# A causal convolution moved from VectorE to TensorE: 72 fp32 products over four token phases

## The chip, the cores and the metric

The kernel runs on one core of one Trainium2 chip, in one launch. The metric is the device time of a run in microseconds (us). One execution of each kernel is also recorded by the hardware profiler; all durations below come from that one execution.

## The reference, cut to what matters

The reference is a small decoder: 512 tokens, 1024 channels, two attention layers, then a block that mixes three kinds of token mixers, then an MLP. The change touches one of the three mixers, the convolution module. Its input `u` is 512 tokens by 512 channels:

```python
def conv_module(u, cv_w, cv_b, ln_w, ln_b):
    a, b = jnp.split(u, 2, axis=-1)
    h = a * jax.nn.sigmoid(b)                       # 512 tokens x 256 channels
    h = lax.conv_general_dilated(h, cv_w[:, None, :], window_strides=(1,),
        padding=[(CV_WIDTH_FILTER - 1, 0)],         # 31 taps, causal
        dimension_numbers=('NWC', 'WIO', 'NWC'),
        feature_group_count=CV_WIDTH) + cv_b        # each channel by itself
    hf = h.astype(f32)
    mu = jnp.mean(hf, axis=-1, keepdims=True)
    var = jnp.mean(jnp.square(hf - mu), axis=-1, keepdims=True)
    hf = (hf - mu) * lax.rsqrt(var + EPS) * ln_w + ln_b
    return jax.nn.silu(hf)
```

The result is concatenated with that of the two other mixers (a gated linear recurrence with four heads, and a sparse attention with four heads) and goes through one output matrix of 1024 by 1024.

## The kernel before, in words

Every large product is done as three fp32r products on TensorE: both operands are split in a high and a low part (`wh`/`wl` for weights, by `load_group` on lines 250 to 268; ScalarE casts `wh`, and VectorE or GpSimd subtracts for `wl`). Weights arrive in 512 KB pieces `raw` on SyncE's DMA queue, with three `raw` buffers and four of each `wh` and `wl`.

The mixers' part of the kernel is written as units: Python generators that issue a piece of work each. The list `ORDER` (line 1182) says in which order the units are issued: `iq`, `sv`, `sN`, `tN` (scores and top-k selection of the sparse attention), `fN`, `vN` (gates and values of a pair of recurrence heads), `hN` (one recurrence head, nine levels, each a chain of VectorE, GpSimd, ScalarE and TensorE), `cu` (projection to the convolution's input, `glu`), `cN` (convolution of channel half N), `sqk` and `dN` (queries and keys, then attention for a pair of heads), `ln` (layer norm and silu of the convolution). The framework then fixes one static order of instructions for each engine out of this list by priority and expected readiness, so that instructions of several units alternate on an engine; on the chip each engine goes through its own list in order, and an instruction that waits holds up all that stands behind it on that engine.

The convolution before (`u_cv`, lines 1141 to 1152): channels are on the partitions, 512 tokens along the free axis, in two halves of 128 channels. A half is one multiplication by the last tap (line 1148) and 30 instructions of multiply and add on VectorE (line 1151, recorded as line 118, which is the helper `stt`), each over 482 to 511 tokens, and a ScalarE instruction that adds the bias (line 1152). `u_ln` (line 1154) transposes the result to tokens on the partitions (`ptc`, eight transposes), takes mean and variance there, transposes back (`ptd`) and applies the silu.

Buffers that matter: tag `s8` has 12 buffers of 8 KB a partition, tag `s4` 7 buffers of 4 KB, tag `w2` 7 of 2 KB, tag `pt` 3 buffers (the probabilities `PT` of the attention and `AT` of a recurrence head share them), and the PSUM tag `mm` three banks. Helpers that record many operations on one line: line 111 and 112 (`ts`), 115 (`tt`), 118 (`stt`), 273 to 275 (the three products of `mm3`).

## Time and profile before

| what | value |
|---|---|
| median of 3 runs | 1347.48 us (1343.02 to 1352.38) |
| the profiled execution's own time | 1343.12 us |
| its span, first to last instruction | 1341.3 us |
| TensorE busy / VectorE busy / ScalarE busy / GpSimd busy | 1237.7 / 843.4 / 586.7 / 355.6 us |
| mean granted TensorE clock | 0.97 of full speed |

The profile cuts the span in 40 slices of 33.5 us; each digit of the busy line is the busy share of a slice in tenths. In the rows further down, times are us from the start of the span unless marked ns. The operation `cv<-glu,cols,cv` is the convolution. A bracket at the end of a timeline row gives the idle time of the engine before the row, and what ended it. Some fp32 products appear as two MATMUL records each: a head's ten products `Oh` of line 1046 give 20 records, a transpose gives one.

### The profile page before, as it was taken

To read this page: it belongs to the slowest core of one execution; us is meant where nothing else is said; L and a number is where in the kernel's file an instruction comes from. 1 tells how busy PE (TensorE), PEld (TensorE's weight loads), DVE (VectorE), ACT (ScalarE), POOL (GpSimd) and SP (SyncE) were. 2 spreads that over 40 slices of the span, in tenths; PEclk is the share of its full clock that TensorE was granted. 3 is DMA by queue.
4 is the path that set the end of the run, shared out by engine and by line. 5 is a ranking of instruction groups with operands and counts; after the bars stand their busy time and mean duration, and the time that the engine had idled before them with its cause. 6 is when DMAs were issued, how large, how long until landed. Compare 5 with 4: busy or idle time off the path is not lost.

```text
span 1341.3 us, 18014 instructions
## 1 busy us (share of the span) xinstructions
PE 1237.7 (92%) x6596; PEld 1010.0 (75%) x6596; DVE 843.4 (63%) x1638; ACT 586.7 (44%) x1196; POOL 355.6 (27%) x434
## 2 busy tenths in 40 slices
PE   5999998999999989999987787988999999999997
PEld 4677777878877868889765666766797888888886
DVE  5647656766467689544899889876586244353444
ACT  4544553553256656326564334644352322131222
POOL 1304202110134240003475755245111010015211
PEclk9999999999999999999999888978999999999999
DMA  5234325424441244343222201030364233234221
GB/s 199 66 124 132 124 96 160 144 70 145 162 134 61 67 142 152 92 144 111 64 69 93 78 18 63 23 108 1 110 219 158 81 124 104 85 110 156 95 79 64
DMA packets 42024, 141.73 MB, mean 106 GB/s; under 512 B 4928, under 2 KB 5824, under 8 KB 41936
## 3 DMA queue, kind: packets, MB, share of 16 engines
q1 hardware_dynamic: 36144, 126.06, 29.0%
q10 hardware_dynamic: 5792, 14.52, 3.1%
q8 instruction: 52, 0.85, 0.3%
q14 instruction: 36, 0.29, 0.1%
HBM read 132.14 MB, written 8.42 MB: 105 GB/s over the span
## 4 chain that ended last, share of the span: by engine, by line
PE 51%; DVE 16%; issue 6%; POOL 5%; ACT 3%; DMA 2%; ACTq 0%; POOLq 0%; DVEq 0%
PE psw L275 4%; PE psw L273 4%; PE psw L274 4%; PE psf L275 4%; PE psf L273 4%; PE psf L274 4%; DVE X L115 2%; PE pso L274 2%; PE pso L275 2%; PE pso L273 2%; PE psg L275 2%; POOL wl L115 2%; PE O L554 2%; PE psg L274 2%; PE psg L273 2%
## 5 line engine op out<-in xcount | busy, mean ns | idle before, releaser
L259 ACT ACTIVATE wh<-raw 128x1024 fp32r<-128x1024 f32 (+2 forms) x138 | 141.9, 1036 | 158.5 <-PE psw L275 50.5
L115 DVE TENSOR_TENSOR wl<-raw,wh 128x1024 fp32r<-128x1024 f32 x104 | 129.8, 1261 | 58.9 <-ACT wh L259 56.7
L115 POOL TENSOR_TENSOR wl<-raw,wh 128x1024 fp32r<-128x1024 f32 (+2 forms) x34 | 76.9, 2281 | 49.4 <-ACT wh L259 49.2
L115 POOL TENSOR_TENSOR hnr<-hnr,mhalf 128x8 f32<-128x8 f32 (+1 forms) x28 | 49.6, 1771 | 152.3 <-DVE hnr L111 141.5
L1261 POOL TENSOR_SCALAR acth<-sqf 128x512 fp32r<-128x512 f32 x32 | 22.9, 718 | 240.3 <-DVE sqf L115 240.3
L274 PE MATMUL psf<-xfl,wh 128*128 128x512 f32 (+1 forms) x232 | 85.5, 369 | 0.4 <-DVE xfl L118 0.4
L275 PE MATMUL psf<-xfh,wl 128*128 128x512 f32 (+1 forms) x232 | 85.3, 368 | 0.1
L273 PE MATMUL psf<-xfh,wh 128*128 128x512 f32 (+1 forms) x232 | 84.5, 367 | 0.0
L273 PE MATMUL psw<-wh,acth 128*128 128x512 f32 (+1 forms) x206 | 79.0, 383 | 0.0
L275 PE MATMUL psw<-wh,actl 128*128 128x512 f32 (+1 forms) x206 | 78.9, 383 | 0.0
L274 PE MATMUL psw<-wl,acth 128*128 128x512 f32 (+1 forms) x206 | 78.9, 383 | 0.0
L519 ACT ACTIVATE PT<-ptp 128x512 f32<-128x512 f32 (+3 forms) x96 | 45.6, 481 | 43.9 <-PE ptp L548 30.8
L336 DVE CUSTOM_DVE_ANT_0 adaw<-adaw,cact 128x1024 f32<-128x1024 f32 x48 | 58.3, 1230 | 5.0 <-DMA adaw<-in_ada 4.8
L511 ACT ACTIVATE P<-Sp,nm 128x128 f32<-128x128 f32 (+3 forms) x80 | 44.5, 557 | 30.5 <-DVE nm L509 30.2
L273 PE MATMUL psq<-wh,xah 128*128 128x512 f32 x128 | 53.2, 415 | 0.9 <-ACT xah L294 0.9
L275 PE MATMUL psq<-wh,xal 128*128 128x512 f32 x128 | 53.2, 415 | 0.2 <-DVE xal L115 0.2
L274 PE MATMUL psq<-wl,xah 128*128 128x512 f32 x128 | 52.9, 413 | 0.0
L118 DVE SCALAR_TENSOR_TENSOR cv<-glu,cols,cv 128x482 f32<-128x482 f32 (+29 forms) x60 | 50.9, 848 | 0.5
L275 PEld LDWEIGHTS psf<-xfh,wl 128*128 128x128 f32 x232 | 43.7, 188 | 7.9 <-DVE wl L115 0.8
L274 PEld LDWEIGHTS psf<-xfl,wh 128*128 128x128 f32 x232 | 43.7, 188 | 7.9 <-DVE xfl L118 0.6
L273 PEld LDWEIGHTS psf<-xfh,wh 128*128 128x128 f32 x232 | 43.5, 188 | 7.2
L554 PEld LDWEIGHTS O<-v,PT 128*128 128x128 f32 x320 | 42.7, 192 | 7.6 <-ACT PT L519 5.4
(522 smaller groups left out, 3596.3 us busy)
## 6 DMA issues: line engine op xcount, KB each, us to landing
raw<-in_w SPq DMA_DIRECT2D x56, 512.0 KB, 3.6
adaw<-in_ada SPq DMA_DIRECT2D x48, 512.0 KB, 4.2
raw<-in_wa SPq DMA_DIRECT2D x32, 512.0 KB, 4.3
raw<-in_w2m SPq DMA_DIRECT2D x32, 512.0 KB, 4.5
raw<-in_wb SPq DMA_DIRECT2D x16, 512.0 KB, 4.7
ck<-cd ACTq DMA_DIRECT2D x16, 256.0 KB, 4.3
raw<-in_woa SPq DMA_DIRECT2D x8, 512.0 KB, 4.9
raw<-in_wob SPq DMA_DIRECT2D x8, 512.0 KB, 4.4
```

The lines of the kernel that those rows point to most:

```text
L115: return note(eng, eng.tensor_tensor(o, x, y, op=op))
L118: return note(ve, ve.scalar_tensor_tensor(o, x, s, y, op0=op0, op1=op1, **kw))
L259: i = ac.activation(wh, r, AF.Copy), tt(gp if len(res) in (gpa if gpl is None else gpl) else ve, wl, r, wh.bitcast(F32), ALU.subtract)
L273: te.matmul(o, lh, rh, start=i == 0, stop=False)
L274: te.matmul(o, lh, rl, start=False, stop=False)
L275: te.matmul(o, ll, rh, start=False, stop=i == n - 1)
L336: i = ve.tensor_tensor_reduce(w, w, ada["c"], 1.0, 0.0, op0=ALU.mult, op1=ALU.add, accum_out=mod[:, j:j + 1])
L511: ac.activation(P[:, :n], Sp[:, :n], AF.Exp, bias=nm, scale=-1.0, accum_out=l)
L519: ac.activation(o, i, AF.Copy)
L554: te.matmul(O[:, i, s], PT[s][:, j], v[:, j, (2 * p + s) * 64:(2 * p + s + 1) * 64], start=j == 0, stop=j == i)
L1261: gp.tensor_scalar(xh, s, 1.0, 0.0, op0=ALU.mult, op1=ALU.add)
```

## The change

The convolution becomes products on TensorE. Tokens are split in four phases (token = 4t + r) and channels in eight groups of 32. For one group, the partitions hold (phase r, channel c), and the free axis holds t, with eight columns of zeros in front: this is `gph`. A product takes 128 consecutive columns of `gph` as the stationary operand, and a table `T` as the moving one: `T` has, for four consecutive tap positions, the tap of channel c on the diagonal of a 32 by 32 block and zeros elsewhere. Nine such products, summed in PSUM, give all 31 taps for 128 t, four phases and 32 channels; eight groups make 72 products. The result has tokens on the partitions, so the layer norm reads it without the eight `ptc` transposes.

- `conv_consts` (new unit `xc`, after `t2`): zeroes on GpSimd, 16 small DMAs on SyncE's queue that write the taps shifted by phase (`wtap`), a scaling by 0.5 and the 32-wide identity `id32` on GpSimd, two transposes on TensorE and a ScalarE copy for the bias row.
- `u_cu`: `glu` is written by phase, and 16 DMAs on SyncE's queue carry it to `gph`.
- `u_cv(m)`: called with m = 1 first, as before; the first call builds `tap8` on VectorE; each call builds four tables `T` of 128 x 1024 on VectorE, issues 36 products into one `mm` bank, and adds the bias on VectorE.
- `u_ln`: no `ptc`; statistics from SBUF, the result of the normalisation in place.
- `ORDER`: `xc` is added; `c0` and `ln` stand earlier.

```diff
@@ -1062,7 +1062,30 @@
         yield
 
     siw = const.tile([128, 4, 8], F32, name="siw")
-    svw = qst = kst = glu = sqk = cv = None
+    svw = qst = kst = glu = sqk = cv = tap8 = None
+
+
+    cvx = S8([128, 2048], F32, "cvx")
+    gph = cvx[:, 0:1088].rearrange("p (g t) -> p g t", t=136)
+    wtap = cvx[:, 1088:1376].rearrange("p (g x) -> p g x", x=36)
+    brow = cvx[:, 1376:1632].rearrange("p (m c) -> p m c", c=128)
+    id32 = cvx[:, 1632:1664]
+
+    def conv_consts():
+        gp.memset(gph[:, :, 0:8], 0.0)
+        gp.memset(wtap, 0.0)
+        o = COLS["cvw"][0]
+        for r in range(4):
+            for q in range(4):
+                sy.dma_start(wtap[32 * r:32 * r + 32, q:8:4, 5 - r:36 - r],
+                             a["cols"][32 * q:32 * q + 32, o:o + 62].rearrange("p (m j) -> p m j", j=31))
+        gp.tensor_scalar(wtap, wtap, 0.5, 0.0, op0=ALU.mult, op1=ALU.add)
+        tt(gp, id32, idc[:, 0:32], idc[:, 32:64], ALU.add)
+        pt = PM("ptm", (128, 4, 128), "tt")
+        for m in range(2):
+            te.transpose(pt[:, m], col("cvb", m).to_broadcast([128, 128]), ident)
+        ac.activation(brow, pt[:, 0:2], AF.Copy)
+
 
     def u_sv():
         nonlocal svw
@@ -1105,7 +1128,7 @@
         nonlocal glu
 
         wc = load_group(a["w2"][1], gpl=gpc)
-        glu = S4([128, 2, 512], "glu")
+        glu = S4([128, 2, 4, 128], "glu")
         psa = []
         for m in (2, 3, 0, 1):
             ps = PM("psc")
@@ -1115,7 +1138,11 @@
                 ac.activation(t, ps, AF.Tanh, scale=0.5)
                 psa.append(t)
             else:
-                stt(glu[:, m], psa[m], 1.0, ps, ALU.add, ALU.mult)
+                v = lambda x: x.rearrange("p (t r) -> p t r", r=4)
+                stt(glu[:, m].rearrange("p r t -> p t r"), v(psa[m]), 1.0, v(ps), ALU.add, ALU.mult)
+        for r in range(4):
+            for q in range(4):
+                sy.dma_start(gph[32 * r:32 * r + 32, q:8:4, 8:136], glu[32 * q:32 * q + 32, :, r])
 
     def u_sqk():
         nonlocal sqk
@@ -1138,48 +1165,51 @@
             mix_out(1, p, pt.rearrange("p a b -> p (a b)"))
             yield
 
-    def u_cv(ms=(0, 1)):
-        nonlocal cv
+    def u_cv(m):
+        nonlocal cv, tap8
 
         if cv is None:
-            cv = S4([128, 2, 512], "cv")
-        for m in ms:
-            w0 = COLS["cvw"][0] + 31 * m
-            ts(ve, cv[:, m], glu[:, m], cols[:, w0 + 30:w0 + 31], ALU.mult)
-            for j in range(30):
-                d = 30 - j
-                stt(cv[:, m, d:512], glu[:, m, 0:512 - d], cols[:, w0 + j:w0 + j + 1], cv[:, m, d:512], ALU.mult, ALU.add)
-            ac.activation(cv[:, m], cv[:, m], AF.Identity, bias=col("cvb", m), scale=0.5)
+            cv = S4([128, 4, 8, 32], "cv")
+            tap8 = S4([128, 8, 4, 32], "tap8")
+            tt(ve, tap8, wtap[:, :, 32:36, None].to_broadcast([128, 8, 4, 32]),
+               id32[:, None, None, :].to_broadcast([128, 8, 4, 32]), ALU.mult)
+        ps = PM("pcv", (128, 4, 4, 32))
+        for g in range(4):
+            gg = 4 * m + g
+            T = S4([128, 32, 32], "taps")
+            tt(ve, T, wtap[:, gg, 0:32, None].to_broadcast([128, 32, 32]), id32[:, None, :].to_broadcast([128, 32, 32]),
+               ALU.mult)
+            for u in range(9):
+                w = T[:, 4 * u:4 * u + 4] if u < 8 else tap8[:, gg]
+                te.matmul(ps[:, g].rearrange("p a b -> p (a b)"), gph[:, gg, u:u + 128], w.rearrange("p a b -> p (a b)"),
+                          start=u == 0, stop=u == 8)
+        bias = brow[:, m].rearrange("p (g c) -> p g c", c=32)
+        tt(ve, cv[:, :, 4 * m:4 * m + 4].rearrange("p q g c -> p g q c"), ps,
+           bias[:, :, None, :].to_broadcast([128, 4, 4, 32]), ALU.add)
 
     def u_ln():
-        ct = S4([128, 4, 256], "ct")
-        for q in range(2):
-            pt = PM("ptc", (128, 2, 2, 128), "tt")
-            for t2 in range(2):
-                for m in range(2):
-                    tb = 2 * q + t2
-                    te.transpose(pt[:, t2, m], cv[:, m, tb * 128:(tb + 1) * 128], ident)
-            for t2 in range(2):
-                tb = 2 * q + t2
-                st = SM(6, "bst")
-                x = pt[:, t2].rearrange("p a b -> p (a b)")
-                ve.bn_stats(st, x)
-                mv = SM(2, "bmv")
-                ve.bn_aggr(mv, st)
-                rr = rstd(mv[:, 1:2], 1, "rrc")
-                ts(ve, ct[:, tb], x, mv[:, 0:1], ALU.subtract, rr, ALU.mult)
+
+        ct = cv.rearrange("p q g c -> p q (g c)")
+        for q in range(4):
+            st = SM(6, "bst")
+            ve.bn_stats(st, ct[:, q])
+            mv = SM(2, "bmv")
+            ve.bn_aggr(mv, st)
+            rr = rstd(mv[:, 1:2], 1, "rrc")
+            ts(ve, ct[:, q], ct[:, q], mv[:, 0:1], ALU.subtract, rr, ALU.mult)
         for m in range(2):
             pt = PM("ptd", (128, 4, 128), "tt")
-            for tb in range(4):
-                te.transpose(pt[:, tb], ct[:, tb, m * 128:(m + 1) * 128], ident)
+            for q in range(4):
+                te.transpose(pt[:, 3 - q], ct[:, q, m * 128:(m + 1) * 128], ident)
             zz = W2("zz")
-            ac.activation(zz, pt.rearrange("p a b -> p (a b)"), AF.Identity, bias=col("lnb", m), scale=col("lnw", m))
+            ac.activation(zz.rearrange("p (t q) -> p q t", q=4), pt, AF.Identity, bias=col("lnb", m),
+                          scale=col("lnw", m))
             th = W2("th")
             ac.activation(th, zz, AF.Tanh, scale=0.5)
             stt(zz, th, 1.0, zz, ALU.add, ALU.mult)
             mix_out(1, 2 + m, zz, 0.5)
 
-    ORDER = "iq sv s2 s3 f0 f0 f0 s1 v0 v0 t2 f1 f1 f1 cu h1 h1 t3 h0 h1 h0 c1 sqk h1 h0 t1 sqk h0 v1 d1 d1 d1 d1 d1 d0 v1 d0 d0 d0 c0 h2 h2 h2 ln h3 d0 h3 h3 h2 h3".split()
+    ORDER = "iq sv s2 s3 f0 f0 f0 s1 v0 v0 t2 xc f1 f1 f1 cu h1 h1 t3 h0 h1 h0 c1 sqk h1 h0 t1 sqk h0 v1 c0 d1 d1 d1 d1 d1 d0 v1 d0 d0 d0 ln h2 h2 h2 h3 d0 h3 h3 h2 h3".split()
... 
     g1 = mod_row(2, "g1")
```

## Rows read from the trace of the kernel before

**Rows 1.** The page, first part: busy time, share of the span, instructions.

```profile
PE 1237.7 (92%) x6596; PEld 1010.0 (75%) x6596; DVE 843.4 (63%) x1638; ACT 586.7 (44%) x1196; POOL 355.6 (27%) x434
```

**Rows 2.** Stretches: us; busy PE, PEld, DVE, ACT, POOL; clock, DMA share, GB/s.

```profile
787.00:839.00 52.00, 40.84 (x224) 32.91 (x224) 46.46 (x72) 20.57 (x47) 24.60 (x29) 0.84 0.13 41
839.00:890.00 51.00, 45.62 (x261) 37.04 (x260) 42.38 (x86) 29.41 (x81) 13.75 (x18) 0.90 0.26 83
890.00:942.00 52.00, 42.85 (x363) 32.47 (x362) 34.83 (x76) 25.19 (x62) 28.69 (x36) 0.84 0.01 4
```

**Rows 3.** Chain that ended last, shares by line: of 787:839, then of 890:942.

```profile
by line: DVE cv L118 30.5%; DVE X L115 12.1%; PE psA L1035 7.9%; PE psA L993 5.3%; PE Oh L1046 4.3%; DVE hhr L111 4.3%; DVE Qs L118 3.8%; DVE KLs L118 3.8%; POOL X L115 3.5%; PE pshi L275 3.4%; PE pt L458 2.9%; PE pshi L273 2.6%; PE pshi L2
...
by line: DVE X L115 28.2%; issue 14.3%; PE psA L993 10.3%; PE Oh L1046 5.6%; DVE D L1020 5.5%; POOL hhr L115 3.9%; PE psA L1035 3.3%; DVE xm L118 3.1%; DVE zz L118 2.6%; ACT sq L1053 2.4%; PE psA L1030 2.2%; PE psA L1025 2.1%; PE pso L275 1
```

**Rows 4.** Groups on VectorE, 640:960: xcount | busy us, mean ns | idle before.

```profile
L118 DVE SCALAR_TENSOR_TENSOR cv<-glu,cols,cv 128x482 f32<-128x482 f32 (+29 forms) x60 | 50.9, 848 | 0.5
...
L115 DVE TENSOR_TENSOR wl<-raw,wh 128x1024 fp32r<-128x1024 f32 x6 | 7.2, 1215 | 0.5 <-ACT wh L259 0.5
...
L115 DVE TENSOR_TENSOR on<-Oh,gg 128x512 f32<-128x512 f32 x4 | 2.7, 685 | 0.1
...
L111 DVE TENSOR_SCALAR cv<-glu,cols 128x512 f32<-128x512 f32 x2 | 1.0, 476 | 0.0
```

**Rows 5.** Timeline of TensorE, 812:836: start, duration, record, idle before.

```profile
816.16 0.65 PE L1025 MATMUL psA<-X 128*64 128x64 f32 x8 [3.25 <-DVE X L115]
...
822.63 0.40 PE L274 MATMUL pshi<-wl,xch 128*128 128x512 f32 x1
822.86 0.40 PE L275 MATMUL pshi<-wh,xcl 128*128 128x512 f32 x1
...
828.87 2.05 PE L1035 MATMUL psA<-X 128*128 128x256 f32 x4 [4.46 <-DVE X L115]
...
831.14 0.63 PE L273 MATMUL pshi<-wh,xch 128*128 128x512 f32 x1
831.57 0.63 PE L274 MATMUL pshi<-wl,xch 128*128 128x512 f32 x1
```

**Rows 6.** Timeline of TensorE: products of a recurrence head at full clock.

```profile
803.20 0.83 PE L1046 MATMUL Oh<-qv,OFF 128*128 128x128 f32 x6
803.87 0.39 PE L1046 MATMUL Oh<-qv,AT 128*128 128x128 f32 x2
```

**Rows 7.** Timeline of GpSimd, 811:829.

```profile
813.05 2.61 POOL L115 TENSOR_TENSOR wl<-raw,wh 128x1024 fp32r<-128x1024 f32 x1
...
822.90 5.54 POOL L115 TENSOR_TENSOR wl<-raw,wh 128x1024 fp32r<-128x1024 f32 x2
```

**Rows 8.** Timeline of VectorE, 811:829.

```profile
813.38 2.31 DVE L111 TENSOR_SCALAR hhr<-hs 128x4 f32<-128x4 f32 x1
...
826.17 2.56 DVE L115 TENSOR_TENSOR X<-qv,X 128x256 f32<-128x256 f32 x1
```

**Rows 9.** Timeline of TensorE at 914, the output matrix.

```profile
914.83 0.50 PE L273 MATMUL pso<-wh,xm 128*128 128x512 f32 x1 [3.01 <-ACT xm L901]
```

**Rows 10.** Waits, 700:950: engine, line, waited for; total us, times, longest.

```profile
POOL AT L984 <- ACT PT L519: 11.1, 1, 11.1
...
PE psc L275 <- POOL wl L115: 7.0, 4, 3.1
```

**Rows 11.** Groups on GpSimd, 600:960.

```profile
L112 POOL TENSOR_SCALAR sg<-sg 128x512 f32<-128x512 f32 x4 | 7.7, 1920 | 13.0 <-DVE la L111 12.9
...
L451 POOL TENSOR_SCALAR KHs<-KHs 64x256 fp32r<-64x256 f32 x8 | 3.3, 408 | 27.5 <-ACT KHs L443 27.5
```

**Rows 12.** SyncE's queue, an issue at the start.

```profile
1.17 0.43 SPq L128 DMA_DIRECT2D ident<-in_const  x1
```

**Rows 13.** SyncE's queue, 760:780.

```profile
762.94 8.90 SPq L256 DMA_DIRECT2D raw<-in_w  x4
```

**Rows 14.** DMA issues: count, KB each, median us to landing.

```profile
raw<-in_w SPq DMA_DIRECT2D x56, 512.0 KB, 3.6
```

More of the change, by code (lines that the diff above doesn't have):

```diff
@@ L1198, in decoder_kernel @@
         k, n = w[0], int(w[1]) if w[1].isdigit() else None
-        if w in ("cu", "iq", "sv", "ln"):
-            {"cu": u_cu, "iq": u_iq, "sv": u_sv, "ln": u_ln}[w]()
+        if w in ("cu", "iq", "sv", "ln", "xc"):
+            {"cu": u_cu, "iq": u_iq, "sv": u_sv, "ln": u_ln, "xc": conv_consts}[w]()
         elif w == "sqk" or k in "fvhd":
@@ L1209, in decoder_kernel @@
         else:
-            u_cv((n,))
+            u_cv(n)
     g1 = mod_row(2, "g1")
```

## The prediction

> **What bounds the kernel now.** I began with the busy times of the page: TensorE is busy for 1237.7 us of the 1341.3 us span, so it bounds the kernel as a whole and VectorE (843.4 us) does not [rows 1]. That average covers unlike stages, so next I looked at the three stretches in which the convolution and the layer norm after it run [rows 2]. From 787 to 839 VectorE is busy for 46.5 of 52 us, TensorE for 40.8, and TensorE's granted clock is only 0.84 on average. From 839 to 890 TensorE leads again (45.6 of 51, clock 0.90). From 890 to 942, the last two recurrence heads, TensorE has 42.9 of 52 at 0.84.
>
> The chain that ended last agrees: from 787 to 839 the convolution on VectorE is its largest part, 30.5%, or 15.9 us. From 890 to 942 the recurrence's `X` leads (28.2%), and the convolution's tail still holds 5.7% through `xm L118` (3.1%) and `zz` (2.6%), or 3.0 us [rows 3].
>
> The timeline shows how VectorE's lateness reaches TensorE. TensorE stands still for 3.25 us and for 4.46 us, both times for a VectorE `X`; before that its products of 512 columns follow each other every 0.23 us, after it every 0.43 us [rows 5]. That is 2.4 and 1.2 GHz: TensorE had been idle when the clock fell. So in this stretch one late VectorE instruction costs TensorE twice.
>
> **The change part by part.**
>
> *Removed from VectorE:* 60 instructions at 848 ns = 50.9 us and 2 at 476 ns = 1.0 us, together 51.9 us [rows 4].
>
> *Added to VectorE:* nine tables of 128 x 1024 (eight `T`, one `tap8`). The trace has no instruction with this broadcast pattern; the nearest of that size is `wl`, two operands, 1215 ns: 9 x 1.22 = 11.0 us. Two bias sums over 512 elements from PSUM, like `on`, at 685 ns: 1.4 us [rows 4]. VectorE ends 51.9 - 12.4 = 39.5 us lighter. Bounds on a table: the 848 ns of a step of the old convolution over half as many elements from below, and from above 1.22 us plus the wait for a whole GpSimd subtraction, which the next paragraph shows, 1.22 + 2.6 = 3.8 us. So 7.6 to 34 us for the nine; I take 11.0, since `wl` has the same size and operand count.
>
> GpSimd's `wl` runs from 813.05 for 2.61 us; a VectorE instruction on four columns that starts at 813.38 takes 2.31 us and ends with it. Two more `wl` from 822.90 take 5.54 us, and an `X` of 256 columns started at 826.17 takes 2.56 us, again to about their end [rows 7, 8]. That is why a table can cost 3.8 us, and also why the 4.46 us wait of TensorE would not vanish just because the convolution does: the `X` that was late was itself held up by `wl`. What vanishes is the queue in front of `X`, with which it could have run before 822.90.
>
> The Trainium skill ("SBUF — State Buffer", section "Who interferes with whom") speaks against the change here: a VectorE instruction with two SBUF operands and a GpSimd instruction that reads SBUF share a port pair by an exclusive lock, and the second one waits for the whole of the first. The tables have two SBUF operands each, so they stay exposed as the old steps were. The trace agrees, with the 2.31 us for four columns. By the rule at its worst the sum would be 8 x 2.6 = 21 us worse on VectorE than I take; the slower rival below has that as a mechanism of its own.
>
> *Added to TensorE:* 72 fp32 products of 128 columns. The rows of `Oh` are of the same form and type and come as two records a product; six records take 803.87 - 803.20 = 0.67 us, 0.112 us each at full clock [rows 6]. So 144 x 0.112 = 16.1 us. At half clock it is twice that, 32 us, as the 0.23 and 0.43 us of rows 5 stand to each other. The eight transposes `ptc` go and two for the bias come; at one such record each, that is -6 x 0.112 = -0.7 us. I take +15.4 us, about 8 of it for each channel half.
>
> *GpSimd:* two memsets, a scaling of 288 columns and a sum of 32. A scaling costs between the 408 ns of `KHs` (256 columns) and the 1920 ns of `sg` (512) [rows 11]; about 1.5 us in all. The scaling waits for 16 DMAs: issue at 0.43 us each [rows 12], 6.9 us, and landing some 3.6 us later [rows 14], so up to 10.5 us. Behind it on GpSimd's queue stand the `wl` of the projection, for which TensorE already waits 7.0 us [rows 10]. Whether the wait is covered depends on where the static order puts it. Bounds 0 to 10; I take 0, because the taps depend on nothing but constants and can be sent long before.
>
> *SyncE:* another 16 issues for `gph`, 6.9 us, behind a wait for `glu`. The next weights, those of the second pair of heads' values, are issued from 762.94 [rows 13], and `wl` of them starts at 813.05 [rows 7]. That is 50 us of cover, so I count 0; without it, 6.9 us. PSUM: the convolution holds one of three `mm` banks for 36 products; 0, at most one evacuation of 0.7 us each time [rows 4].
>
> *ScalarE* loses two bias instructions and gains one copy; it is at 20.6 of 52 us [rows 2], so 0.
>
> **Sum, stretch by stretch, against TensorE, the one that is late next.**
>
> 787 to 839: TensorE was granted 0.84 x 52 = 43.7 us of full-speed time and idled 52 - 40.8 = 11.2 us. If the idle time fell at half clock, its work is 43.7 - 5.6 = 38.1 us at full speed; if at full clock, 32.5. With 8 us of convolution the stretch could shrink to between 40.5 and 46.1 us: -11.5 to -5.9. I take -9. (By the chain alone it would be -15.9, so TensorE takes some 7 of it back.)
>
> 839 to 890: the same way 0.90 x 51 = 45.9, idle 5.4, work 40.5 to 43.2, plus 8: 48.5 to 51.2, so -2.5 to +0.2. I take -1. TensorE was the bound here already.
>
> 890 to 942: the layer norm moves ahead of the last heads; the 3.0 us of its tail on the chain go, as does the 3.01 us for which TensorE waits for `xm` [rows 9], and 0.9 us of `ptc`. These overlap; I take -4. The heads themselves do not start earlier: GpSimd waits 11.1 us for a `pt` buffer that the attention still holds [rows 10], and that stays.
>
> Together -14: 1343.1 - 14 = 1329 us for an execution like the profiled one. The median of the three runs, 1347.48, lies 4.4 us above the profiled one; I put half of that back: **1331 us**.
>
> **Rivals.**
>
> *TensorE takes it all back (same).* TensorE is at 92% and the change adds 15.4 us to it. If the clock's dips and the waits come from `wl` and the heads' own chain rather than from the convolution, nothing but the queue is freed: the chain's 15.9 us go, 15.4 come. 1343 to 1348. For it: the 2.31 us of rows 8. Against it: VectorE is nearly full in the stretch.
>
> *TensorE waits for tables (slower).* In the code, seven `s4` buffers face `svw`, `posm`, `gg`, two `OFF`, `cv`, `tap8`: all seven, while the first two heads live. Then a table has no second buffer: each of the eight groups waits for its build, and everything behind it on TensorE's queue with it. Price: eight times 1.22 us plus half a `wl`, 8 x 2.5 = 20 us, and the convolution at half clock, another 16 us, instead of the gain: -14 + 20 + 16 = +22, 1365, or 1367 with the 2 us above. It decides when the waits and the clock together cost over 14 us, that is 1.8 us a group. Against it: other products can be ordered in between, and a buffer is free once a head ends.
>
> *More is freed (much faster).* In the three stretches TensorE loses 0.16 x 52 + 0.10 x 51 + 0.16 x 52 = 21.7 us to the clock and idles 25.7 us [rows 2]. If VectorE's relief also shortened the heads' chains so far that all of it went, -47.4 + 15.4 = -32, or 1311 (1313 with the 2 us above). For it: `X` holds 12 and 28% of the chain in two of them. Against it: some idle time lies at half clock and is counted twice here.
>
> That the change does not do what it says I rule out: the 62 instructions are gone from the source.
>
> **How the numbers follow.** A difference of about 1% (13.5 us) is what this measurement can tell from none. Forecast 0.50 (1318 to 1340), taken back 0.30, slower 0.13, much faster 0.07. Below 1334 lie about 0.43 of the forecast's 0.50 and the 0.07: faster 0.50. Same: the forecast's other 0.07, all of the second case, and a little of the third's 0.13: 0.38. Slower: 0.12. The range from 1313 to 1354 leaves out part of the last two cases.
>
> **What would show it.** Right: no `cv L118`; VectorE some 40 us lighter; `Oh`-like records of 0.11 us, 144 of them; TensorE's clock in these slices nearer to 1.0 and its waits for `X` shorter; the stretch to `xm` of the convolution ends earlier. Wrong: TensorE rows with waits for a `taps` table or for a DMA into `gph`; GpSimd idle before the scaling with TensorE waiting for `psc`; the convolution's records at 0.215 us; or the last heads starting no earlier than now after the same total of waits.

## The result: 8.7 us slower, where 14 us less were forecast

| | before | after |
|---|---|---|
| median | 1346.18 us (1339.82 to 1352.38, 11 runs) | 1353.96 us (1350.46 to 1359.65, 11 runs) |
| ratio | | 1.0065, 95% interval 1.0041 to 1.0089 |
| the profiled execution's own time | 1343.12 us | 1351.38 us |
| its span | 1341.3 us | 1349.6 us |

The loss is below the 1% that the forecast called "same", yet outside the interval of no change: the kernel became 5.5 to 12 us slower. The 8.7 us of the heading are 0.0065 of 1346 us; the two medians themselves differ by 7.8. 1331 us was not reached by far: 1353.96 stands at the upper edge of the forecast's range (1313 to 1354). Two executions of the experiments below, one of 1519.82 us (e5_swapfew) and one of 3918.26 us (e14_midg), stand far apart from all others and are in no ratio, and the first is the profiled one, so no trace of e5_swapfew is read.

The busy line of the page after, to be read beside [rows 1]:

```profile
PE 1245.7 (92%) x6734; PEld 1024.8 (76%) x6734; DVE 804.4 (60%) x1587; ACT 586.7 (43%) x1195; POOL 353.6 (26%) x438
```

VectorE is 39.0 us lighter, as worked out, and nothing of it arrives at the end. Where it went is seen when both kernels are cut into the same stretches. The columns are those of [rows 2]. First the kernel before, then after:

```profile
740.00:797.00 57.00, 45.33 (x349) 33.85 (x349) 47.93 (x102) 19.60 (x32) 41.12 (x50) 0.82 0.15 47
797.00:839.00 42.00, 34.29 (x169) 28.48 (x168) 41.08 (x62) 18.08 (x42) 18.55 (x15) 0.88 0.16 51
839.00:885.00 46.00, 42.09 (x245) 34.36 (x244) 37.73 (x78) 28.57 (x79) 9.57 (x13) 0.89 0.18 55
885.00:940.00 55.00, 44.44 (x366) 33.66 (x365) 39.49 (x82) 24.27 (x59) 32.86 (x42) 0.84 0.10 35
```

```profile
740.00:797.00 57.00, 36.15 (x329) 29.90 (x329) 47.36 (x100) 18.93 (x30) 40.36 (x50) 0.76 0.18 56
797.00:839.00 42.00, 40.44 (x240) 33.94 (x241) 17.91 (x38) 19.54 (x43) 14.01 (x16) 1.00 0.07 19
839.00:885.00 46.00, 42.84 (x257) 35.95 (x256) 20.91 (x50) 19.42 (x57) 10.76 (x9) 0.96 0.11 34
885.00:940.00 55.00, 44.78 (x412) 35.10 (x410) 39.54 (x83) 29.19 (x64) 32.65 (x44) 0.94 0.23 77
```

From 797 to 885 the picture is the forecast one. VectorE falls from 41.1 to 17.9 of 42 us, TensorE's clock rises from 0.88 to 1.00, and the two waits for `X` of [rows 5] are gone. What TensorE waited for from 797 to 885, before and then after (line, waited for, us in total, times, longest):

```profile
PE psA L1035 <- DVE X L115: 4.5, 1, 4.5
PE psA L1025 <- DVE X L115: 3.3, 1, 3.3
```

```profile
PE pth L1060 <- ACT on L1057: 2.6, 2, 2.5
PE psA L1025 <- DVE X L115: 0.8, 1, 0.8
```

The loss lies ahead of that, before the first product of the convolution has run: from 740 to 797 TensorE is busy for 36.2 us where it was busy for 45.3, at a lower clock (0.76 for 0.82). What is missing there is `psqk`, the 96 products that make queries and keys of the attention. Here are their last line of three, the last product of the attention and the first product of the MLP, as groups of TensorE's timeline up to 1000 (count, ns min/median/max, first and last start in us), before and after:

```profile
L275 PE MATMUL psqk<-wh,xcl x32: 388/389/796, 770.1 to 821.5; 128*128 128x512 f32 x32
...
L554 PE MATMUL O<-svw,PT x80: 217/275/474, 849.5 to 885.0; 128*128 128x64 f32 x80
...
L273 PE MATMUL psf<-xfh,wh x38: 274/283/384, 977.3 to 999.1; 128*128 128x256 f32 x38
```

```profile
L275 PE MATMUL psqk<-wh,xcl x32: 387/389/476, 805.9 to 834.2; 128*128 128x512 f32 x32
...
L554 PE MATMUL O<-svw,PT x80: 218/275/471, 864.7 to 901.0; 128*128 128x64 f32 x80
...
L273 PE MATMUL psf<-xfh,wh x24: 274/283/284, 985.5 to 999.7; 128*128 128x256 f32 x24
```

Before, these products were spread from 763 to 821 and filled TensorE while it waited for the two recurrence heads. After, the first of them starts right behind the convolution's first half, as TensorE's timeline shows:

```profile
797.45 1.95 PE L1184 MATMUL pcv<-taps,cvx 128*128 128x128 f32 x16
799.23 0.39 PE L1184 MATMUL pcv<-tap,cvx 128*128 128x128 f32 x2
...
805.26 0.39 PE L1184 MATMUL pcv<-tap,cvx 128*128 128x128 f32 x2
805.40 0.47 PE L273 MATMUL psqk<-wh,xch 128*128 128x512 f32 x1
```

Their own inputs were there: the last `wl` of their weights starts on GpSimd at 769.65 and takes 2.36 us. The row of `pcv` carries no wait either. What held `psqk` up is the static order, in which it stands behind `pcv`; and `pcv` stands late there, since the first table is built on VectorE only at 795.56. So 9 us of TensorE's work leave a stretch in which it idles and go, with 16 us of new products, into 797 to 885, where it is then busy for 83.3 of 88 us.

The small terms, from the groups of VectorE (755 to 880) and SyncE's queue after:

```profile
L115 DVE TENSOR_TENSOR taps<-cvx 128x1024 f32<-128x1024 f32 x8 | 10.3, 1298 | 1.9 <-PE pcv L1184 1.9
L118 DVE SCALAR_TENSOR_TENSOR glu<-tc,psc 128x512 f32<-128x512 f32 x2 | 2.1, 1050 | 0.0
...
L115 DVE TENSOR_TENSOR cv<-pcv,cvx 128x512 f32<-128x512 f32 x2 | 1.4, 692 | 6.0 <-PE pcv L1184 6.0
L115 DVE TENSOR_TENSOR tap<-cvx 128x1024 f32<-128x1024 f32 x1 | 1.2, 1220 | 0.0
```

```profile
763.46 3.50 SPq L256 DMA_DIRECT2D raw<-in_w  x2
767.07 10.70 SPq L1145 DMA_DIRECT2D cvx<-glu  x16
777.87 1.01 SPq L256 DMA_DIRECT2D raw<-in_w  x2
```

Tables and bias sums cost what was worked out. The 16 issues for `gph` took 10.7 us, not 6.9, and put the next two weights off to 777.87, but their first cast on ScalarE comes only at 830.63: covered, as said.

### The profile page after: what moved, and what is told of

The parts are those of the page before. It is cut to its first block, busy times and chain, and to the rows that moved or that the text cites. A ratio compares the mean times of both kernels' runs of the same rounds, so it can differ in the third digit from the quotient of the medians.

```text
span 1349.6 us, 18319 instructions
## 1 busy us (share of the span) xinstructions
PE 1245.7 (92%) x6734; PEld 1024.8 (76%) x6734; DVE 804.4 (60%) x1587; ACT 586.7 (43%) x1195; POOL 353.6 (26%) x438
## 4 chain that ended last, share of the span: by engine, by line
PE 54%; DVE 13%; POOL 6%; issue 5%; ACT 3%; DMA 2%; POOLq 0%; ACTq 0%; SPq 0%; DVEq 0%
PE psw L274 4%; PE psw L275 4%; PE psw L273 4%; PE psf L274 4%; PE psf L275 4%; PE psf L273 4%; PE pso L274 2%; PE pso L275 2%; PE pso L273 2%; DVE X L115 2%; PE O L554 2%; PE psg L274 2%; PE psg L275 2%; PE psg L273 2%; POOL wl L115 2%
## 5 line engine op out<-in xcount | busy, mean ns | idle before, releaser
L273 PE MATMUL psf<-xfh,wh 128*128 128x512 f32 (+1 forms) x232 | 84.5, 367 | 0.0
L274 PE MATMUL pso<-wl,ogh 128*128 128x512 f32 x120 | 47.0, 392 | 0.5 <-DVE wl L115 0.4
```

The lines of the kernel that those rows point to most:

```text
L273: te.matmul(o, lh, rh, start=i == 0, stop=False)
L274: te.matmul(o, lh, rl, start=False, stop=False)
```

## The experiments

Fifteen kernels ran, each timed against the kernel before, whose medians beside them were 1342 to 1344 us; only the ratios are compared across them. Theory from the trace above: the convolution's PSUM bank, `pcv`, has the tag `mm` like that of `psqk`; banks of a tag are handed out in the order of the list, and `c1` stands ahead of `sqk` in it. In the kernel before that order cost nothing, since the convolution on VectorE took no bank.

All their profiles are read by the same three marks, the last starts of `psqk` and of `O<-svw`, and the first of `psf`. The table is what the sections below refer to; "1st", "mid", "last" say into which of the three spans a half of the convolution falls (V: on VectorE). Times are us; where a half straddles a mark both spans are named.

| kernel | ratio | last `psqk` | to last `O` | to first `psf` | halves |
|---|---|---|---|---|---|
| before | 1 | 821.5 | 63.5 | 92.3 | V: 1st/mid, mid/last |
| after | 1.0065 | 834.2 | 66.8 | 84.5 | 1st, mid |
| e1_swap | 1.0018 | 831.7 | 63.2 | 83.5 | 1st, mid |
| e2_tt | 1.0032 | 832.5 | 62.8 | 84.9 | 1st, mid |
| e3_few | 0.9985 | 832.1 | 60.6 | 84.5 | 1st, mid, 16 products |
| e4_hold | 1.0037 | 827.3 | 65.6 | 88.1 | V: 1st/mid |
| e6_lastc | 1.0003 | 825.3 | 56.0 | 97.0 | mid/last, last |
| e7_mid | 0.9997 | 822.3 | 64.1 | 90.9 | mid, mid/last |
| e8_oldpos | 1.0059 | 835.5 | 56.5 | 92.4 | 1st, mid/last |
| e9_notaps | 0.9927 | 824.2 | 54.9 | 88.0 | 2 of 30 steps a half |
| e10_swapo | 1.0030 | 834.7 | 54.9 | 92.5 | 1st, mid/last |
| e13_swapg | 1.0004 | 832.9 | 59.1 | 84.7 | 1st, mid, fp32r |
| e14_midg | 1.0009 | 824.1 | 64.0 | 89.9 | mid, mid/last, fp32r |
| e15_lastcg | 1.0010 | 818.1 | 60.4 | 97.8 | mid/last, last, fp32r |

### Is it the order of the list and the bank?

**e1_swap** puts the projection ahead in the list of the kernel after:

```diff
-h0 c1 sqk h1 h0 t1 sqk h0 v1 c0
+h0 sqk c1 h1 h0 t1 sqk h0 v1 c0
```

Expected: 

> The changed kernel with one edit: in ORDER the first sqk stands ahead of c1. Queue theory (the convolution's PSUM bank is taken from the same tag, in the order of the list, so the attention projection psqk cannot start until the convolution's first products can, and TensorE has nothing to do between the head products from 763 to 797): psqk starts near 763 us again instead of 805, TensorE is busy for over 28 of the 40 us from 760 to 800 instead of 22.5, and the time falls by 10 to 20 us to 1334 to 1344. Price theory (the 144 added records on TensorE are what costs): nothing leaves TensorE, so 1350 to 1358. SyncE theory (the 16 transfers of glu ahead of the weights are what costs): they stay, so 1350 to 1358 too.

**e2_tt** leaves the list alone and takes the bank from another tag:

```diff
-        ps = PM("pcv", (128, 4, 4, 32))
+        ps = PM("pcv", (128, 4, 4, 32), "tt")
```

Expected: 

> The changed kernel with one edit: the convolution's bank comes from the PSUM tag tt (two banks, used by transposes) instead of mm; ORDER stays as changed, with c1 ahead of sqk. Queue theory: psqk starts near 763 as in e1 although c1 still stands ahead of it, and the time falls to 1334 to 1346 (transposes now share one bank while the convolution runs, a few us at most). Were the order in the list alone the cause, psqk would still start near 805 and the time stay at 1350 to 1358; so too by the price and the SyncE theory for the time.

**e3_few** leaves list and bank alone and issues 16 of the 72 products (seven of nine tap blocks are left out):

```diff
-            for u in range(9):
+            for u in (0, 8):
```

Expected: 

> The changed kernel with 16 products of the convolution instead of 72 (two of nine for each group: the other seven taps' blocks are left out of the sum); all tables, transfers and the order stay. It takes 56 x 2 x 0.112 = 12.5 us off TensorE. Price theory: the time falls by about 12 us to 1341 to 1344, and that is all of the loss. Queue theory: TensorE still stands idle from 763 to 797 (22 to 24 us busy in 760 to 800) with psqk behind it; psqk starts 6 us earlier, and the time falls by 6 to 13 us, no further than 1341, so still clear of what e1 gives.

**e4_hold** goes the other way. In the kernel before, the first product of `psqk` is ordered on TensorE behind the last `Oh` product of head 1, which puts it about where the kernel after has it:

```diff
-h0 c1 sqk h1 h0 t1 sqk h0
+h0 c1 h1 sqk h0 t1 sqk h0
...
+        hold["dep"] = last["oh", 1]
...
+            if "dep" in hold:
+                after(x, hold.pop("dep"))
```

Expected: 

> The kernel before, convolution on VectorE, with one thing done to it: psqk's first product is ordered on TensorE behind the last output product of head 1 (no wait is added, only the place in the queue), as it stands in the changed kernel. Queue theory: the gap between the heads' products stays empty from 763 to about 797, and the kernel before becomes 10 to 25 us slower, 1356 to 1371, with no convolution on TensorE at all. Price and SyncE theory: nothing of what they blame is there, 1342 to 1350.

Measured: e1_swap 1345.57 us, ratio 1.0018 (0.9995 to 1.0042); e2_tt 1346.85 us, 1.0032 (1.0007 to 1.0057); e3_few 1341.14 us, 0.9985 (0.9958 to 1.0012); e4_hold 1348.18 us, 1.0037 (1.0012 to 1.0062).

The start of the first line of `psqk` in e1_swap, and in e3_few:

```profile
L273 PE MATMUL psqk<-wh,xch x32: 387/389/880, 765.1 to 831.3; 128*128 128x512 f32 x32
```

```profile
L273 PE MATMUL psqk<-wh,xch x32: 387/391/478, 801.9 to 831.6; 128*128 128x512 f32 x32
```

Swapping two words of the list, or naming another bank, brings the start back from 805.4 to 765.1 and 766.3. With the old order and few products it stays at 801.9. So the order sets the start, and neither the products' time nor their inputs do. Its price: 1.0065 - 1.0018 = 0.0047, or 6.3 us, by e1_swap, 4.4 us by e2_tt (alone not clear of the noise, some 4.5 us for the difference of two such ratios), and 5.0 us (1.6 to 8.3) when the same delay is put into the kernel before.

The size was expected too large. e1_swap and e2_tt miss their ranges (1334 to 1344 and to 1346 us), so the order is less of the loss than expected; the price and SyncE theories, which gave 1350 to 1358, are further off. The time of e3_few fits both of its cases, only its start of `psqk` and its 23.8 us of TensorE from 760 to 800 speak for the order. e4_hold missed its 10 us and more: of the delay of 37 us at the first `psqk` (800.4 against 763.2), 5.8 us are left at the last (827.3 against 821.5) and 7.9 us at the end of the attention, of which the last span gives 4.2 us back.

### Do the two prices add, and what is VectorE's relief worth alone?

**e5_swapfew** is e1_swap and e3_few in one. Expected: 

> The projection stands ahead of the convolution in the list (as in e1_swap) and only two of the nine products of each channel group are left (as in e3_few; seven of nine tap blocks are left out of the convolution). Theory (two separate costs, the late projection and 14 us of TensorE time in a full stretch): the two gains add. The kernel as changed stands at ratio 1.0065; the order alone took 0.0047 off, the fewer products alone 0.0080: 1.0065 - 0.0127 = 0.994, so 0.992 to 0.996, attention's queries and keys from about 765, TensorE busy over 15 us in 760 to 780, the end of attention near 886. Rival (both only undo the same lateness of attention): no better than the better one alone, 0.997 to 1.000, the end of attention at 892.

**e9_notaps** is the kernel before with the old convolution cut short, and nothing else:

```diff
-            for j in range(30):
+            for j in range(28, 30):
```

Expected: 

> The kernel before with 2 of the 30 multiply-and-add instructions in each half of the convolution; the other 28 taps of a half are left out. VectorE loses 56 x 0.85 = 47 us and nothing is added anywhere: the relief alone. Theory (VectorE was in the way of little, TensorE or the heads' own chain is late next): 5 to 9 us, ratio 0.993 to 0.996, TensorE's waits for X in 787 to 839 mostly still there. Rival (the forecast's working, by which the stretches from 787 to 942 would give back 14 us net of 15 us of products, so 29 us without products): ratio near 0.978.

Measured: e5_swapfew 1339.13 us, ratio 0.9957 (0.9938 to 0.9977); e9_notaps 1333.18 us, 0.9927 (0.9902 to 0.9953), a little better than its theory and far from its rival. In one point it was wrong: TensorE's waits for `X` were not "mostly still there".

e5_swapfew lies inside the first of its two cases, as it would if the prices add, though its interval reaches into the second. With it the whole difference can be told as a chain of four steps: taking the old convolution off VectorE is worth -0.0073 of 1343 us, **-9.8 us** (e9_notaps). Tables, moving, bias and 16 products cost 0.0030, **+4.0 us** (e5_swapfew against it; that step also holds the earlier place of `c0` and `ln` in the list, and the four steps and two multiplications that e9_notaps keeps). The other 56 products cost 0.0061, **+8.2 us** (e1_swap), for 12.4 us of TensorE's time at 0.222 us each. The order of the banks costs 0.0047, **+6.3 us** (after). The sum is +8.7 us, as it must be, since each step starts where the one before it ends. By the intervals a step is good to 3.4 to 4.5 us, so the +4.0 us alone is not clear of nothing.

The first link is the surprise. In e9_notaps nothing is added anywhere, and VectorE has 45 us less to do (798.7 us busy). Its marks:

```profile
L275 PE MATMUL psqk<-wh,xcl x32: 387/389/797, 773.7 to 824.2; 128*128 128x512 f32 x32
...
L554 PE MATMUL O<-svw,PT x80: 219/275/323, 845.3 to 879.1; 128*128 128x64 f32 x80
...
L273 PE MATMUL psf<-xfh,wh x52: 274/283/397, 967.1 to 998.8; 128*128 128x256 f32 x48, 128*128 128x512 f32 x4
```

The attention ends 5.9 us earlier than before and the span behind it is 4.3 us shorter. That is all. Its rows for the stretches of [rows 2], and its largest wait of TensorE for `X` from 797 to 885:

```profile
787.00:839.00 52.00, 43.24 (x263) 33.92 (x264) 28.71 (x63) 29.36 (x70) 29.40 (x41) 0.90 0.13 44
839.00:890.00 51.00, 46.47 (x346) 37.41 (x344) 25.51 (x63) 26.41 (x67) 15.92 (x21) 1.00 0.24 83
890.00:942.00 52.00, 42.13 (x318) 31.86 (x316) 36.86 (x70) 25.23 (x59) 25.09 (x30) 0.97 0.04 13
```

```profile
PE psA L1025 <- DVE X L115: 0.7, 1, 0.7
```

The clock rose in all three stretches (0.84, 0.90 and 0.84 before). The idle time did not come back: 23.2 us of the 155, against 25.7 before. Of the two waits of [rows 5], 7.7 us, 0.7 us is left.

Behind the attention the gain is not the convolution's tail of [rows 3]: TensorE's wait for `xm` is still there (3.1 us), and from the first `zz` of the chain to the first `psf` it is 65.8 us in both kernels (from 911.5 before, from 901.3 in e9_notaps). What went are three steps of the convolution that stood on VectorE ahead of the last heads' `X`. The chain that ended last, before and then e9_notaps, from the attention's result `onf` on:

```profile
885.34 0.69 DVE onf L115
886.03 1.07 DVE cv L118
...
887.44 0.69 DVE cv L118
...
888.73 0.99 DVE cv L118
889.72 5.29 DVE X L115 x9
```

```profile
879.38 0.69 DVE onf L115
880.07 0.33 DVE D L115
880.40 1.52 DVE X L115 x3
```

In e4_hold the convolution's last step starts at 882.1, ahead of the attention's end at 892.9, and its last span is as short (88.1 us). The waits and these steps (2.8 us) together are near the gain of 9.8 us; that they make it up wait by wait is not shown, and e9_notaps has its last `psqk` 2.7 us later than before.

### Does it matter where the products stand?

All four have fp32 products and all 31 taps; the list alone differs (**e6_lastc** first, then **e7_mid**, **e8_oldpos**, **e10_swapo**):

```diff
-h0 c1 sqk h1 h0 t1 sqk h0 v1 c0 d1 d1 d1 d1 d1 d0 v1 d0 d0 d0 ln h2 h2 h2 h3
+h0 sqk h1 h0 t1 sqk h0 v1 d1 d1 d1 d1 d1 d0 v1 d0 d0 d0 h2 c1 h2 c0 h2 ln h3
+h0 sqk h1 h0 t1 sqk c1 h0 v1 d1 d1 d1 d1 d1 d0 v1 d0 d0 d0 c0 h2 h2 h2 ln h3
+h0 c1 sqk h1 h0 t1 sqk h0 v1 d1 d1 d1 d1 d1 d0 v1 d0 d0 d0 c0 h2 h2 h2 ln h3
+h0 sqk c1 h1 h0 t1 sqk h0 v1 d1 d1 d1 d1 d1 d0 v1 d0 d0 d0 c0 h2 h2 h2 ln h3
```

e6_lastc, expected: 

> The projection ahead, and the convolution as a whole (c1, c0, then ln) among the first levels of the last two recurrence heads, where TensorE waits for the heads' chain. Theory (the price of the products depends on whether TensorE is full where they stand): attention ends near 885 as in the kernel before; of the 16 us of products about half falls into the 9 us that TensorE idles and the slow clock there, so the last stretch, 92 us before, is 92 to 98 us long: ratio 0.999 to 1.004 against 1.0018 with the projection ahead alone; if VectorE's relief also counts, down to 0.996. Rival (the products cost the same wherever they stand): 1.002, with the end of attention earlier by 10 us and the last stretch longer by the same. Second rival (the tables queue ahead of the heads' own VectorE chain, and the normalisation comes too late for the output product): last stretch over 100 us, ratio over 1.007.

e7_mid, expected: 

> The projection ahead, c1 right behind it, c0 and ln among the last heads, as in the kernel before. Theory: half of the products (8 us) leaves the full stretch; attention ends at 888 to 892, the last stretch is 88 to 92 us: ratio 0.997 to 1.002. Rival (the products cost the same wherever they stand): 1.002 as in e1_swap, the end of attention near 891.

e8_oldpos, expected: 

> The kernel as changed, with c0 and ln back where the kernel before has them; c1 still ahead of the projection. Theory (the late projection costs 5 to 6 us by itself): the attention's projection still begins only behind c1, near 800, attention ends at 893 to 897 instead of 901, the last stretch grows from 84 to 88 to 92 us: ratio 1.004 to 1.007. Rival (it was the earlier c0 and ln that cost the time, crowding attention): 0.999 to 1.002.

e10_swapo, expected: 

> The projection ahead, c1 right behind it in the list as in e1_swap, c0 and ln among the last heads as in the kernel before. If the place of c1 in the list matters only through the projection: as e7_mid, 0.998 to 1.001, attention's end 888 to 892. If the second half of the convolution costs the same wherever it stands: 1.002 as e1_swap.

Measured: e6_lastc 1344.05 us, 1.0003 (0.9986 to 1.0021); e7_mid 1345.06 us, 0.9997 (0.9978 to 1.0015); e8_oldpos 1352.33 us, 1.0059 (1.0038 to 1.0079); e10_swapo 1346.81 us, 1.0030 (1.0009 to 1.0052).

e8_oldpos agrees with the first theory and excludes that the earlier `c0` and `ln` were to blame: with both back in place the kernel is as slow as after. e6_lastc lies inside its theory too, with a last span of 97.0 us; so does the time of e7_mid, whose attention ended earlier than expected (886.4). e10_swapo lies nearer to its second case, and against e8_oldpos, with the same places of `c0` and `ln`, it prices the order once more: 0.0029, or 3.9 us, no more than the noise.

For the rest the table is read, by its middle span, from the end of the projection to the end of the attention. Where a whole half in fp32 products stands in it, or one and a half as in e7_mid, it takes 62.8 to 66.8 us (after, e1_swap, e2_tt, e7_mid), and 54.9 to 56.5 us where there is none (e9_notaps) or about half of one (34 to 38 of its 72 records come before the attention's last product in e6_lastc, e8_oldpos and e10_swapo). With the convolution on VectorE it is 63.5 us. The last span takes 83.5 to 84.9 us where all products lie ahead of it (after, e1_swap, e2_tt), 90.9 to 92.5 us with 34 records of a half and the norm (e7_mid, e8_oldpos, e10_swapo), 92.3 us with the end of the convolution and the norm on VectorE, and 97.0 us with 110 of the 144 records and the norm. So a half costs 6 to 12 us in the middle, and half of one with the norm 6 to 9 us at the end; the spans don't tell products, tables and norm apart. It is about as much as the convolution on VectorE cost in the same spans. The expectation that products among the last heads come cheaper, since TensorE idles there, did not hold: what e10_swapo wins in the middle against e1_swap (8.3 us) it loses at the end (9.0 us). The best places only reach a tie with the kernel before.

### Are cheaper products the way out?

**e11_swapr** and **e12_swapor** are e1_swap and e10_swapo with fp32r products; a ScalarE copy rounds the input into a buffer of the 8 KB pool. **e13_swapg**, **e14_midg** and **e15_lastcg** are e1_swap, e7_mid and e6_lastc with the copy in a 4 KB buffer for each half:

```diff
...
+        gr = S4([128, 4, 136], "gr", F32R)
+        ac.activation(gr, gph[:, 4 * m:4 * m + 4], AF.Copy)
...
-            T = S4([128, 32, 32], "taps")
+            T = S4([128, 32, 32], "taps", F32R)
...
-                te.matmul(ps[:, g].rearrange("p a b -> p (a b)"), gph[:, gg, u:u + 128], w.rearrange("p a b -> p (a b)"),
+                te.matmul(ps[:, g].rearrange("p a b -> p (a b)"), gr[:, g, u:u + 128], w.rearrange("p a b -> p (a b)"),
```

e11_swapr, expected: 

> As e1_swap, with the 72 products in fp32r: a ScalarE copy rounds the gathered input into a tile of its own, the tables are written as fp32r. The products round their operands, as one fp32r product does. Theory (the price of the change is TensorE's time in a full stretch): the products take 0.06 to 0.11 us each instead of 0.22, 8 to 12 us of TensorE's time go, and of the 8 us between e1_swap and e5_swapfew most comes back: ratio 0.996 to 0.999. Rival (the price lies in the wait for tables and the queue behind them, not in the products' time): 1.001 to 1.003.

e12_swapor, expected: 

> As e10_swapo with fp32r products. If e11's theory holds and half of the products lies among the last heads: 0.994 to 0.998; else as e10_swapo.

e13_swapg, expected: 

> As e1_swap with fp32r products (operands rounded by ScalarE and VectorE, one record a product, half of TensorE's time), the rounded copy of the input in a small buffer for each channel half. Theory (TensorE's time is the price where it is full): 8 us of TensorE time go from 800 to 880, so 4 to 8 us against e1_swap: 0.996 to 0.999. Rival (the tables and the order are the price): 1.001 to 1.004.

e14_midg, expected: 

> As e7_mid with fp32r products. Theory: half of the saved 8 us lies in the full stretch and counts, the other half among the last heads counts in part: 0.994 to 0.998 against 0.9997. Rival: 0.999 to 1.002.

e15_lastcg, expected: 

> As e6_lastc with fp32r products. Theory: the last stretch, 95 us there, is shorter by part of the 8 us: 0.995 to 0.999 against 1.0003. Rival: 0.999 to 1.002.

Measured: e11_swapr 1353.72 us, 1.0073 (1.0049 to 1.0097); e12_swapor 1355.11 us, 1.0078 (1.0051 to 1.0106); e13_swapg 1341.65 us, 1.0004 (0.9987 to 1.0021); e14_midg 1343.18 us, 1.0009 (0.9990 to 1.0027); e15_lastcg 1343.23 us, 1.0010 (0.9990 to 1.0030).

None of the five reached its theory: the first two are slower than both of their cases, e13_swapg lies between its two, e14_midg and e15_lastcg at their rivals. The first two say nothing of the products' price. In e11_swapr the copy starts only at 816.09 and the convolution at 817.25; the second half of `psqk` stands behind the convolution in TensorE's order, TensorE idles for 6.6 us ahead of both, and the last `psqk` moves to 838.6. That is like the kernel after once more. That the 8 KB pool held the copy up is inferred from e13_swapg, where with 4 KB buffers the convolution starts at 803.6.

The other three have one record a product instead of two and so 8 us less of TensorE's time than their partners, yet they gain 1.9 us at e13_swapg, within the intervals, and nothing at the other two. They also add two ScalarE copies (0.66 us each in e13_swapg). Two things are seen in their traces. In e13_swapg TensorE now catches up with the tables; its timeline:

```profile
807.52 1.11 PE L1186 MATMUL pcv<-taps,gr 128*128 128x128 f32 x8 [0.66 <-DVE taps L115]
...
812.24 1.11 PE L1186 MATMUL pcv<-taps,gr 128*128 128x128 f32 x8 [0.83 <-DVE taps L115]
```

And in e15_lastcg the attention ends at 878.5, 6.5 us before that of the kernel before, but TensorE then has the clock of 0.55 from 880 to 900, and the products follow each other every 0.21 us, where in e13_swapg it is 0.12 (the columns of the first row are those of [rows 2]):

```profile
880.00:900.00 20.00, 16.72 (x149) 15.68 (x147) 19.00 (x30) 7.09 (x13) 13.05 (x15) 0.55 0.00 1
```

```profile
894.43 1.91 PE L1186 MATMUL pcv<-taps,gr 128*128 128x128 f32 x8
896.13 0.41 PE L1186 MATMUL pcv<-tap,gr 128*128 128x128 f32 x1
```

VectorE is at 19.0 of 20 us there: tables (5.6 us) and the heads' first levels want it at once. So the price of a half is not TensorE's time alone. How it divides into products, tables and what they push aside stays open: 56 products of 0.222 us cost 8.2 us between e5_swapfew and e1_swap, while halving the time of all 72 gave back 1.9 us at best.

No version with all 31 taps is faster than the kernel before; the best tie with it.

## Why the prediction was wrong

**Right.** VectorE: 39.5 us forecast, 39.0 measured. A table 1.22 us forecast, 1.30 on average. A bias sum 685 ns forecast, 692 measured. A record of the new products 0.112 us forecast: 16 of them from 797.45 to 799.23, 0.111 each. GpSimd's and SyncE's parts were covered. The waits for `X` went and the clock rose to 1.00 in that stretch, as the list of signs said. The last two heads did not start earlier relative to the attention: GpSimd's `X` of theirs starts at 900.7, against 884.8 before, and the attention's last product at 901.0 against 885.0, and GpSimd still waits for the attention there (1.6 us ahead of its last `AT`), so the buffer of [rows 10] still rules. The last stretch gained: 84.5 us for 92.3, -7.8 us where -4 was forecast (the convolution's last steps left it, too); TensorE's wait for `xm` fell from 3.0 to 1.3 us there.

**The step that failed first** is the sentence on PSUM: "the convolution holds one of three `mm` banks for 36 products; 0, at most one evacuation of 0.7 us each time". It asked how long a bank is held, and not who is next in line for it. The list puts `c1` ahead of `sqk`, the bank order follows the list, and so 96 products that needed nothing from the convolution had to wait for it. This costs 4 to 6 us (6.3 by e1_swap, 5.0 by e4_hold, 4.4 by e2_tt, 3.9 between e10_swapo and e8_oldpos, the last two not clear of the noise by themselves).

**The step that was mis-sized most** is the stretch sum, "-11.5 to -5.9, I take -9" for 787 to 839 and "-1" for the next. It took TensorE's idle time and its slow clock in a stretch as time that comes back once VectorE is free. Without the products' 15.4 us the working claims 25 us for the first two stretches, and 4 more for the norm, which e9_notaps does not move; e9_notaps measured 9.8 us (6.3 to 13.2). The clock did rise (0.90, 1.00 and 0.97 for 0.84, 0.90 and 0.84), and the idle time did not come back: 23.2 us of the 155 for 25.7, with VectorE 45 us lighter. What VectorE's lateness put on TensorE's path, as far as the traces show it, were the two waits of [rows 5] and three steps of the convolution ahead of the last heads. The idle time that is left belongs mostly to the heads' chain and the norm's: in e9_notaps from 787 to 942 the largest waits in total are 4.9 us for the heads' `on` from ScalarE, 3.8 us for `xm` and 3.5 us for the heads' `X` from GpSimd.

**The rival** that came nearest is "TensorE takes it all back", 1343 to 1348, with a chance of 0.30. e1_swap is that case in its time (1345.57 us, 1.0018), and by the chain of steps its sum is near: -9.8 us of relief, +12.2 us of new work. Its condition is not met: by it the clock's dips and the waits do not come from the convolution, and both were mostly gone without it. The kernel after is this rival and 6 us of queue order on top. The slower rival had the right place and another mechanism: TensorE does stand behind the convolution, but it waits for no table there (the rows of `pcv` carry no wait).

**The shared port.** The rule of the Trainium skill that the prediction weighed ("SBUF — State Buffer", section "Who interferes with whom") did not decide here: the tables of the kernel after took 1.22 to 1.76 us each, nowhere the 3.8 us of the upper end, and by its worst case the loss would have stood in TensorE's waits for tables, of which its rows show none. Of the rows that the prediction set beside the rule, only the `X` of 2.56 us has two operands in SBUF; the instruction of 2.31 us [rows 8] adds a constant to one, so it is no case of what the rule says of two.

## What to carry to other kernels

Before new work gets a buffer or a PSUM bank from a shared tag, look at who takes the next one in program order and whether that one has been filling idle time; a word's place in an issue list, or another tag, can be worth as much as the change itself. Idle time and a slow clock of the bounding engine in a stretch are not a gain that waits for whoever is busy there: the waits that end on the engine to be relieved are the better guide (here 7.7 us of waits and 2.8 us of steps in the way, for a measured relief of 9.8; the stretch sum said 25). Cheapest of all is to try the relief alone, with the old work cut out and nothing put in its place; when that gives 10 us, a replacement that takes 16 us of the bounding engine has little left to win: here its work cost 12.2 us.

## What was not expected of the hardware

`glu` written by phase, with a stride of 512 bytes between neighbouring elements of a row, took 1.05 us on VectorE; written in order it took 0.68 us before, for the same 512 elements a partition. Issues of the 16 small copies between partitions took 0.6 to 0.9 us each on SyncE's queue (10.7 us in all), against the 0.43 us of [rows 12] and 0.33 us for a weight. An fp32 product of 128 columns is two records of 0.111 us, the fp32r product of the same size one record of 0.11 to 0.12 us (eight from 807.52 to 808.47 in e13_swapg). And a higher clock in a stretch is no sign of a faster kernel: TensorE's clock from 797 to 885 was 0.98 in the kernel that lost and 0.88 in the one that won. The delay of `psqk` is not what raised it, since it is 0.98 in e1_swap, without the delay, and 0.91 in e4_hold, with the delay alone.
